# A trunk of two layers on one core: the recurrence's keys normed together behind its query projections, and the second layer's maps folded behind a feed-forward round

## The chip, the cores and the metric

The kernel runs on one core of one Trainium2 chip. The metric is the device time of one execution in microseconds. Names used here: PE is TensorE, DVE is VectorE, ACT is ScalarE, POOL is GpSimd, and SP is SyncE, whose queue issues nearly all transfers. L425 is line 425 of the kernel before.

## The reference, cut to what matters

Input is one sequence of 512 tokens of width 1024. Layer 0 norms it and projects it once; the columns go to a sparse attention (an indexer scores all keys and keeps the best 128 per query) and to a recurrence (RWKV-7). The part that is moved here belongs to the recurrence:

```
u = token_shift(u, mu)
r, k, v, xw, xa, xg = _split_cols(u, B_COLS)
a = jax.nn.sigmoid(a0 + xa @ a2)
kk = heads(k * k_k)
kk = kk / jnp.maximum(jnp.linalg.norm(kk, axis=-1, keepdims=True), 1e-12)
k = k * (1.0 + (a - 1.0) * k_a)
```

Here r are the recurrence's queries, k its keys and v its values, 512 columns each, in 8 heads of 64. A delta rule over the tokens follows. The two mixers' results are concatenated and projected, and a SwiGLU feed-forward and a per-layer embedding follow. Layer 1 has another mixer (mLSTM): an up-projection, a convolution over four tokens, small block-diagonal maps to queries, keys and values, and gates that are linear in those. The maps and the gates' weights multiply into combined maps that depend on weights alone. Layer 1 has a feed-forward and an embedding of its own.

## The kernel before, in words

Activations are kept turned, as 128 features by 512 tokens, one tile per 128 features, in an arena of 69 equal buffers that are handed out first in, first out (take, takes, give). A projection (project, L206 on) makes one tile of 128 outputs: eight input tiles times three matmuls, 24 in all, because weights and activations are each split into a high and a low part and three of the four products are summed. For each four input tiles, weights (L176) loads 256 KB on SP into one of four buffers, ACT casts the high part (L182) and POOL or DVE subtracts it to get the low part (L183) in one of three buffers; it is POOL in the first layer's mixer and DVE in the feed-forward. DVE takes the result from PSUM (L425), and shifted (L428) adds the previous token with one ACT and one DVE operation (L432, L433).

in_proj (L437) runs the recurrence's preparation. Before the change it went through the four key tiles one by one, with the next tile's projection started ahead: key(j, ks), L480 to L501, squares the tile on ACT (L483), sums the squares of each head on PE, turns the sums (one copy, L277, and one transpose), takes the reciprocal root with two ACT functions and one refinement step on DVE (rsqrt_act, L252 to L257, on 128x8 values), spreads it over the head's 64 rows by an ACT copy and four PE transposes (spread, L281 on; the copy is L286), and multiplies on DVE (L494 to L497) while POOL makes other products (L493, L499, L500). When all four are done, pairs_ab (L749) multiplies keys and rates, sends the result through memory (16 writes on SP, L760, one read, L762), and solve (L764) inverts blocks with 30 dependent DVE operations. The four query tiles (r) were projected after the solve in the text, each used and given back at once (L524 to L528, with DVE's bonus product L527).

The selection of the best keys (choose, L594) is 16 rounds of two DVE operations (L600, L601) and a last comparison (L603) for each of three query tiles, with a much later priority: fillers. The first 24 rounds are free to run once the scores are there, the others stand behind the solve's last operation.

From there rwkv (L854) writes the order of PE's groups out by hand, with group and issue_after. Everywhere else the order on each engine is made by the framework's scheduler: it simulates the program with its own durations and takes, for each engine, the ready instruction with the earliest place in the text. The engines then run that order strictly. issue_after(ins) orders what a block issues on the engine of ins behind ins, and nothing on other engines.

fold_maps (L1139 to L1187) makes layer 1's combined maps: two loads on SP (L1145, L1147), two dozen DVE operations (L1154 to L1172), a write to memory and a read back (L1174, L1178), a split and two POOL masks. It is called from layer 0's feed-forward (ffn, L1417) ahead of its third round (j = 2), a round being a gate and an up projection, DVE's evacuations (L1426, L1428), their product (L1429) and its split (L187, L188).

The last group norm of the recurrence (r_norm, L1075 on) is among PE's hand-ordered groups; the first half of the output projection (mixes, with ya) runs around it, and the second half (out_proj, with yb) needs its result.

Of the kernel before, what the change touches and what calls it, by code (L numbers as in the profile page):

```python
# [9 lines left out]
F32 = mybir.dt.float32  # L10
F32R = mybir.dt.float32r
I32 = mybir.dt.int32
AF = mybir.ActivationFunctionType
OP = mybir.AluOpType
# [4 lines left out]
P = 128  # L19
# [7 lines left out]
NT = S // P  # L27
# [18 lines left out]
def tl(c, n=P):  # L46
    return slice(c * n, (c + 1) * n)


class Trunk:  # L50
# [386 lines left out]
    def in_proj(self, ikw, *iq):  # L437
        nc, a = self.nc, self.a
        lora = self.takes(2)
        nc.sync.dma_start(lora[0], a["lora_w"])  # L440
        nc.sync.dma_start(lora[1], a["lora_a"])
        g2 = self.take()
        nc.sync.dma_start(g2, a["g2"])

        self.ikw, self.iq = ikw, iq

        wa = self.shifted(12)
        nc.scalar.activation(wa[0:64], wa[0:64], AF.Tanh)
        self.scores()
        xg = self.shifted(13)  # L450
        sg, av = self.takes(4), self.takes(4)
        sigmoids = []
        for j in range(4):
            ps = self.aux("decay")
            nc.tensor.matmul(ps, lora[0][:, tl(j)], wa, start=True, stop=True)
            sigmoids.append(nc.scalar.activation(sg[j], ps, AF.Sigmoid, bias=self.vec("w0", j)))
            ps = self.aux("a")
            nc.tensor.matmul(ps, lora[1][:, tl(j)], wa, start=True, stop=True)
            sigmoids.append(nc.scalar.activation(av[j], ps, AF.Sigmoid, bias=self.vec("a0", j)))
        sigmoids.append(nc.scalar.activation(xg, xg, AF.Sigmoid))  # L460

        with ExitStack() as ctx:
            for i in sigmoids:
                ctx.enter_context(self.tc.issue_after(i.ins))
            last = nc.scalar.preload_act_table_set("natural_log_exp_and_others")
        self.give(*lora, wa)
        inv = self.takes(4)
        dec = sg
        for j in range(4):
            nc.vector.tensor_tensor_scan(sg[j], self.reset, sg[j], 0.0, OP.mult, OP.add)  # L470
        with self.tc.issue_after(last.ins):
            for j in range(4):
                nc.scalar.activation(inv[j], sg[j], AF.Exp, scale=EXP_HALF)
                nc.scalar.activation(dec[j], sg[j], AF.Exp, scale=-EXP_HALF)
                nc.scalar.copy(self.PL[:, :, j], dec[j].rearrange("p (n t) -> p n t", t=64)[:, :, 63])
        self.give(self.reset)

        self.KK, self.Bt, self.Kt = [], [], []

        def key(j, ks):  # L480
            d3 = dec[j].rearrange("p (n t) -> p n t", t=64)
            sq = self.take()
            nc.scalar.activation(sq, ks, AF.Square, scale=self.vec("kk", j))  # L483
            ps = self.sums([[sq[:, tl(c)]] for c in range(NT)], self.heads)
            self.give(sq)
            v = self.sm.tile([P, 8], F32, name="kkv", tag="kkv")
            nc.vector.tensor_scalar(v.rearrange("p (c n) -> p c n", n=2), ps[:, :, :2], 1e-24, None, op0=OP.max)
            pb = self.spread(self.rsqrt_act(v, 8, "rk").rearrange("p (c n) -> p c n", c=NT), nc.scalar.copy)
            kk, bt, kt = self.takes(3)
            self.KK.append(kk)  # L490
            self.Bt.append(bt)
            self.Kt.append(kt)
            nc.gpsimd.tensor_tensor(bt, av[j], inv[j], op=OP.mult)  # L493
            nc.vector.scalar_tensor_tensor(kk, pb, self.vec("kk", j), ks, op0=OP.mult, op1=OP.mult)  # L494
            nc.vector.tensor_tensor(bt, kk, bt, op=OP.mult)
            k3 = kk.rearrange("p (n t) -> p n t", t=64)
            nc.vector.tensor_tensor(k3[:, :, 1:], k3[:, :, 1:], d3[:, :, :-1], op=OP.mult)  # L497
            nc.vector.tensor_scalar(av[j], av[j], self.vec("ka", j), self.ka1[:, j:j + 1], op0=OP.mult, op1=OP.add)
            nc.gpsimd.tensor_tensor(av[j], av[j], ks, op=OP.mult)  # L499
            nc.gpsimd.tensor_tensor(kt, av[j], inv[j], op=OP.mult)  # L500
            self.give(ks)  # L501

        ks = self.shifted(4)
        for j in range(4):
            k, ks = ks, self.shifted(5 + j) if j < 3 else None
            key(j, k)
        self.give(*inv)
        self.pairs_ab()

        self.kept = kept = []  # L510
        last = self.solve()
        with self.later(LATER):
            for c in range(1, NT):
                for i in range(17):
                    if (c, i) < (2, 8):
                        self.choose(c, i)
                    else:
                        with self.tc.issue_after(last.ins):
                            self.choose(c, i)
        self.kept = None  # L520
        keys = self.keys_in()
        next(keys)

        for j in range(4):  # L524
            rs = self.shifted(j)
            nc.gpsimd.tensor_tensor(self.Rt[:, j], rs, dec[j], op=OP.mult)
            nc.vector.scalar_tensor_tensor(self.bonus[:, j], rs, self.vec("rk", j), av[j], op0=OP.mult, op1=OP.mult)  # L527
            self.give(rs)  # L528
            if j == 1:
                next(keys, None)  # L530
        self.give(*dec, *av)
        vs = [self.shifted(8 + j) for j in range(4)]

        for j in range(4):
            gp = self.aux("gate")
            nc.tensor.matmul(gp, g2[:, tl(j)], xg, start=True, stop=True)
            bp = self.aux("bonus")
            bo, gate = self.bonus[:, j], self.gate[:, j]
            nc.tensor.matmul(bp, self.hblk, bo, start=True, stop=True)
            nc.vector.tensor_tensor(bo, bp, vs[j], op=OP.mult)  # L540
            nc.scalar.copy(gate, gp)
            nc.vector.scalar_tensor_tensor(bo, bo, self.vec("gnb", j), gate, op0=OP.add, op1=OP.mult)
            nc.scalar.mul(gate, gate, self.vec("gng", j))
        self.give(xg, g2)

        self.V = []
        for c in range(NT):
            ps = self.aux("vtok")
            for j in range(4):
                nc.tensor.matmul(ps[:, tl(j)], vs[j][:, tl(c)], self.center, start=True, stop=True)  # L550
            self.V.append(self.take())
            nc.scalar.copy(self.V[c], ps)
        self.give(*vs)
        self.give(*kept)
        self.q = [self.taken(17 + i) for i in range(4)]
# [861 lines left out]
    def ffn(self, i, after):  # L1417
        nc, a = self.nc, self.a
        h = []
        for j in range(NH):  # L1420
            if (i, j) == (0, 2):
                self.fold_maps()
            pg = self.project(a["ffn_w_gate"][i, j], self.xhi, self.xlo)
            pu = self.project(a["ffn_w_up"][i, j], self.xhi, self.xlo)
            gt, ut = self.takes(2)
            nc.vector.tensor_tensor(gt, pg, self.rstd, op=OP.mult)  # L1426
            nc.scalar.activation(gt, gt, AF.Silu)
            nc.vector.tensor_tensor(ut, pu, self.rstd, op=OP.mult)  # L1428
            nc.vector.tensor_tensor(ut, ut, gt, op=OP.mult)  # L1429
            hi, lo = self.pair("h")  # L1430
            self.split(hi, lo, ut)
            self.give(gt, ut)
            h.append((hi, lo))
        self.norm_done()
        self.norm_begin()
        for m in range(KD):
            ps = self.project(a["ffn_w_down"][i, m], *zip(*h))
            nc.vector.tensor_tensor(self.x[m], self.x[m], ps, op=OP.add)
            self.norm_tile(m, after)
        self.norm_end()  # L1440
        for hl in h:
            self.give(*hl)
# [169 lines left out]
```

## Time and profile before

| what | us |
|---|---|
| median of 3 runs | 1614.05 |
| lowest and highest | 1612.14, 1614.37 |
| the profiled execution's own time | 1613.23 |
| its span, first to last instruction | 1611.1 |

How it is read: the page's first part gives each engine's busy share of the span. A table of stretches gives the same for parts of the span, with TensorE's mean granted clock (1.00 is 2.4 GHz, 0.50 is 1.2 GHz). The view of waits says which engine idled, at which line, and what released it. The timeline lists instructions in order of time, each with the idle time ahead of it in brackets and what ended it. In all views, out<-in are the names of the tiles written and read; "t" is any arena tile.

### The profile page before, as it was taken

To read this page: it belongs to the slowest core of one execution; us is meant where nothing else is said; L and a number is where in the kernel's file an instruction comes from. 1 tells how busy PE (TensorE), PEld (TensorE's weight loads), DVE (VectorE), ACT (ScalarE), POOL (GpSimd) and SP (SyncE) were. 2 spreads that over 40 slices of the span, in tenths; PEclk is the share of its full clock that TensorE was granted. 3 is DMA by queue.
4 is the path that set the end of the run, shared out by engine and by line. 5 is a ranking of instruction groups with operands and counts; after the bars stand their busy time and mean duration, and the time that the engine had idled before them with its cause. 6 is when DMAs were issued, how large, how long until landed. Compare 5 with 4: busy or idle time off the path is not lost.

```text
span 1611.1 us, 25318 instructions
## 1 busy us (share of the span) xinstructions
PE 1540.2 (96%) x9814; PEld 1245.3 (77%) x9814; DVE 940.0 (58%) x1733; ACT 679.7 (42%) x1242; POOL 309.0 (19%) x288
## 2 busy tenths in 40 slices
PE   8789989989999999999999999999899999999998
PEld 5566767868888888888777777777788888888887
DVE  6988946576444443336676666657655444443345
ACT  5643446534333333334454655354453333333233
POOL 5545220121000000002300325353420000000002
PEclk9999999999999999999999999999999999999999
DMA  4124120222333333343322113121233333333332
GB/s 160 53 53 143 49 68 16 75 81 94 99 98 97 96 96 108 105 119 127 107 90 81 52 54 104 53 70 50 65 105 94 97 98 98 99 92 98 98 99 98
DMA packets 90112, 142.46 MB, mean 88 GB/s; under 512 B 19588, under 2 KB 24708, under 8 KB 89992
## 3 DMA queue, kind: packets, MB, share of 16 engines
q1 hardware_dynamic: 89992, 140.84, 28.6%
q8 instruction: 77, 1.26, 0.3%
q14 instruction: 43, 0.35, 0.1%
HBM read 133.26 MB, written 7.54 MB: 87 GB/s over the span
## 4 chain that ended last, share of the span: by engine, by line
PE 79%; DVE 16%; ACT 2%; issue 2%; DMA 1%; POOL 1%; SPq 0%; DVEq 0%; ACTq 0%; POOLq 0%
PE mm L145 66%; DVE t L601 2%; DVE m L600 1%; DVE t L1399 1%; PE s L145 1%; PE spread L148 1%; PE S L1320 1%; PE num L1367 1%; PE S L1321 1%; PE S L1319 1%; PE num L1368 1%; PE num L1369 1%; PE v L1353 1%; POOL t L1482 1%; PE po L145 1%
## 5 line engine op out<-in xcount | busy, mean ns | idle before, releaser
L145 PE MATMUL mm<-x,whi 128*128 128x512 f32 (+1 forms) x2496 | 780.4, 393 | 3.3 <-ACT x L308 3.3
L145 PEld LDWEIGHTS mm<-x,whi 128*128 128x128 f32 x2496 | 467.9, 189 | 105.7 <-issue 4.7
L182 ACT CAST whi<-wraw 128x512 fp32r<-128x512 f32 (+1 forms) x470 | 284.0, 606 | 572.2 <-PE mm L145 517.2
L145 PE MATMUL mm<-x,wlo 128*128 128x512 f32 (+1 forms) x1248 | 489.7, 392 | 3.4 <-POOL wlo L183 3.4
L183 DVE TENSOR_TENSOR wlo<-wraw,whi 128x512 fp32r<-128x512 f32 x352 | 245.4, 697 | 248.1 <-ACT whi L182 247.6
L145 PEld LDWEIGHTS mm<-x,wlo 128*128 128x128 f32 x1248 | 236.4, 189 | 53.5 <-POOL wlo L183 4.9
L183 POOL TENSOR_TENSOR wlo<-wraw,whi 128x512 fp32r<-128x512 f32 (+1 forms) x118 | 154.6, 1315 | 342.9 <-ACT whi L182 334.6
L145 PE MATMUL mm<-h,whi 128*128 128x512 f32 x704 | 216.8, 389 | 0.0
L318 POOL TENSOR_TENSOR t<-t 128x512 f32<-128x512 f32 x42 | 56.9, 1356 | 759.6 <-ACT t L317 759.3
L145 PEld LDWEIGHTS mm<-h,whi 128*128 128x128 f32 x704 | 132.2, 188 | 27.5
L145 PE MATMUL mm<-h,wlo 128*128 128x512 f32 x352 | 136.9, 389 | 0.0
L145 PE MATMUL mm<-y,whi 128*128 128x512 f32 x256 | 82.8, 402 | 2.8 <-DVE t L1410 2.8
L145 PEld LDWEIGHTS mm<-h,wlo 128*128 128x128 f32 x352 | 66.1, 188 | 13.6
L1428 DVE TENSOR_TENSOR t<-mm,t 128x512 f32<-128x512 f32 x44 | 30.4, 692 | 67.1 <-PE mm L145 67.1
L1426 DVE TENSOR_TENSOR t<-mm,t 128x512 f32<-128x512 f32 x44 | 30.4, 692 | 66.2 <-PE mm L145 64.6
L145 PEld LDWEIGHTS mm<-y,whi 128*128 128x128 f32 x256 | 49.0, 193 | 13.3 <-ACT whi L182 3.2
L187 ACT CAST h<-t 128x512 fp32r<-128x512 f32 x44 | 27.3, 620 | 64.9 <-DVE t L1429 64.9
L145 PE MATMUL mm<-y,wlo 128*128 128x512 f32 x128 | 50.9, 398 | 0.0
L309 DVE SCALAR_TENSOR_TENSOR x<-t,vecs,x 128x512 fp32r<-128x512 f32 x48 | 39.0, 815 | 19.2 <-ACT x L308 19.2
L188 DVE TENSOR_TENSOR h<-t,h 128x512 fp32r<-128x512 f32 x44 | 30.5, 693 | 30.0 <-ACT h L187 29.9
L308 ACT ACTIVATE x<-t,vecs 128x512 fp32r<-128x512 f32 x48 | 34.8, 725 | 27.6 <-POOL t L1482 15.5
L1214 DVE SCALAR_TENSOR_TENSOR t<-t,vecs 128x511 f32<-128x511 f32 (+2 forms) x48 | 35.7, 749 | 6.1 <-ACT t L1212 5.2
(363 smaller groups left out, 1853.2 us busy)
## 6 DMA issues: line engine op xcount, KB each, us to landing
wraw<-in_ffn_w_gate_dram SPq DMA_DIRECT2D x88, 256.0 KB, 2.6
wraw<-in_ffn_w_up_dram SPq DMA_DIRECT2D x88, 256.0 KB, 2.6
wraw<-in_ffn_w_down_dram SPq DMA_DIRECT2D x80, 256.0 KB, 2.6
wraw<-in_c_w_up_dram SPq DMA_DIRECT2D x64, 256.0 KB, 2.6
wraw<-in_w_in_dram SPq DMA_DIRECT2D x38, 256.0 KB, 2.6
wraw<-in_ple_w_gate_dram SPq DMA_DIRECT2D x32, 256.0 KB, 2.6
wraw<-in_c_w_down_dram SPq DMA_DIRECT2D x32, 256.0 KB, 2.7
t<-in_x_dram SPq DMA_DIRECT2D x16, 256.0 KB, 4.5
```

The source lines that it names most:

```text
L145: self.last = self.nc.tensor.matmul(*args, **kw)
L182: nc.scalar.copy(hi, raw)
L183: self.wlo_engine.tensor_tensor(lo, raw, hi.bitcast(F32), op=OP.subtract)
L187: self.nc.scalar.copy(hi, src)
L188: self.nc.vector.tensor_tensor(lo, src, hi.bitcast(F32), op=OP.subtract)
L308: nc.scalar.activation(hi, self.x[m], AF.Identity, scale=g)
L309: nc.vector.scalar_tensor_tensor(lo, self.x[m], g, hi.bitcast(F32), op0=OP.mult, op1=OP.subtract)
L318: nc.gpsimd.tensor_tensor(self.acc, self.acc, sq, op=OP.add)
L601: nc.vector.match_replace(acc, m8, acc, TAKEN)
L1214: nc.vector.scalar_tensor_tensor(xc[:, k:], xm[:, :-k], self.vec("cw", 16 * (3 - k) + i), xc[:, k:], op0=OP.mult, op1=OP.add)
L1426: nc.vector.tensor_tensor(gt, pg, self.rstd, op=OP.mult)
L1428: nc.vector.tensor_tensor(ut, pu, self.rstd, op=OP.mult)
```

## The change

The keys' four tiles are projected one after the other. Their squares are taken together, summed into one PSUM tile, and turned once, after the first query's projection. One reciprocal root of 128x32 values follows, and then two more query projections. Only then come the four spreads, with the products of each key as before. The fourth query's projection stands after them, ahead of the pairs. The four query tiles are held until all are used. Second, the block that calls fold_maps is put behind the last product of the feed-forward's second round (j = 1), so that its DVE operations may not be scheduled before it; its transfers and its ACT and POOL operations are not bound by that.

```
--- before.py
+++ after.py
@@ -477,34 +477,36 @@
 
         self.KK, self.Bt, self.Kt = [], [], []
 
-        def key(j, ks):
+
+        ks = [self.shifted(4 + j) for j in range(4)]
+        sqs = self.takes(4)
+        for j in range(4):
+            nc.scalar.activation(sqs[j], ks[j], AF.Square, scale=self.vec("kk", j))
+        sums = self.sums([[sq[:, tl(c)] for sq in sqs] for c in range(NT)], self.heads, turned=False)
+        self.give(*sqs)
+        rs = [self.shifted(0)]
+        sums = self.turned(sums)
+        v = self.sm.tile([P, 32], F32, name="kkv", tag="kkv")
+        nc.vector.tensor_scalar(v.rearrange("p (c n) -> p c n", n=8), sums[:, :, :8], 1e-24, None, op0=OP.max)
+        v = self.rsqrt_act(v, 32, "rk").rearrange("p (c n) -> p c n", c=NT)
+        rs += [self.shifted(1), self.shifted(2)]
+        for j in range(4):
             d3 = dec[j].rearrange("p (n t) -> p n t", t=64)
-            sq = self.take()
-            nc.scalar.activation(sq, ks, AF.Square, scale=self.vec("kk", j))
-            ps = self.sums([[sq[:, tl(c)]] for c in range(NT)], self.heads)
-            self.give(sq)
-            v = self.sm.tile([P, 8], F32, name="kkv", tag="kkv")
-            nc.vector.tensor_scalar(v.rearrange("p (c n) -> p c n", n=2), ps[:, :, :2], 1e-24, None, op0=OP.max)
-            pb = self.spread(self.rsqrt_act(v, 8, "rk").rearrange("p (c n) -> p c n", c=NT), nc.scalar.copy)
+            pb = self.spread(v[:, :, 2 * j:2 * j + 2], nc.scalar.copy)
             kk, bt, kt = self.takes(3)
             self.KK.append(kk)
             self.Bt.append(bt)
             self.Kt.append(kt)
             nc.gpsimd.tensor_tensor(bt, av[j], inv[j], op=OP.mult)
-            nc.vector.scalar_tensor_tensor(kk, pb, self.vec("kk", j), ks, op0=OP.mult, op1=OP.mult)
+            nc.vector.scalar_tensor_tensor(kk, pb, self.vec("kk", j), ks[j], op0=OP.mult, op1=OP.mult)
             nc.vector.tensor_tensor(bt, kk, bt, op=OP.mult)
             k3 = kk.rearrange("p (n t) -> p n t", t=64)
             nc.vector.tensor_tensor(k3[:, :, 1:], k3[:, :, 1:], d3[:, :, :-1], op=OP.mult)
             nc.vector.tensor_scalar(av[j], av[j], self.vec("ka", j), self.ka1[:, j:j + 1], op0=OP.mult, op1=OP.add)
-            nc.gpsimd.tensor_tensor(av[j], av[j], ks, op=OP.mult)
+            nc.gpsimd.tensor_tensor(av[j], av[j], ks[j], op=OP.mult)
             nc.gpsimd.tensor_tensor(kt, av[j], inv[j], op=OP.mult)
-            self.give(ks)
-
-        ks = self.shifted(4)
-        for j in range(4):
-            k, ks = ks, self.shifted(5 + j) if j < 3 else None
-            key(j, k)
-        self.give(*inv)
+        self.give(*ks, *inv)
+        rs.append(self.shifted(3))
         self.pairs_ab()
 
         self.kept = kept = []
@@ -522,13 +524,11 @@
         next(keys)
 
         for j in range(4):
-            rs = self.shifted(j)
-            nc.gpsimd.tensor_tensor(self.Rt[:, j], rs, dec[j], op=OP.mult)
-            nc.vector.scalar_tensor_tensor(self.bonus[:, j], rs, self.vec("rk", j), av[j], op0=OP.mult, op1=OP.mult)
-            self.give(rs)
+            nc.gpsimd.tensor_tensor(self.Rt[:, j], rs[j], dec[j], op=OP.mult)
+            nc.vector.scalar_tensor_tensor(self.bonus[:, j], rs[j], self.vec("rk", j), av[j], op0=OP.mult, op1=OP.mult)
             if j == 1:
                 next(keys, None)
-        self.give(*dec, *av)
+        self.give(*dec, *av, *rs)
         vs = [self.shifted(8 + j) for j in range(4)]
 
         for j in range(4):
@@ -1419,14 +1419,16 @@
         h = []
         for j in range(NH):
             if (i, j) == (0, 2):
-                self.fold_maps()
+
+                with self.tc.issue_after(mark.ins):
+                    self.fold_maps()
             pg = self.project(a["ffn_w_gate"][i, j], self.xhi, self.xlo)
             pu = self.project(a["ffn_w_up"][i, j], self.xhi, self.xlo)
             gt, ut = self.takes(2)
             nc.vector.tensor_tensor(gt, pg, self.rstd, op=OP.mult)
             nc.scalar.activation(gt, gt, AF.Silu)
             nc.vector.tensor_tensor(ut, pu, self.rstd, op=OP.mult)
-            nc.vector.tensor_tensor(ut, ut, gt, op=OP.mult)
+            mark = nc.vector.tensor_tensor(ut, ut, gt, op=OP.mult)
             hi, lo = self.pair("h")
             self.split(hi, lo, ut)
             self.give(gt, ut)
```

## Rows read from the trace of the kernel before

**Rows 1.** Page, part 1: busy us, share of the span and instructions of each engine
```profile
PE 1540.2 (96%) x9814; PEld 1245.3 (77%) x9814; DVE 940.0 (58%) x1733; ACT 679.7 (42%) x1242; POOL 309.0 (19%) x288
```

**Rows 2.** Stretches: from:to, length, busy of PE, PEld, DVE, ACT, POOL, clock, DMA
```profile
53.80:109.90 56.10, 43.37 (x243) 31.37 (x241) 53.05 (x116) 26.46 (x55) 31.59 (x27) 0.91 0.17 52
109.90:130.40 20.50, 19.89 (x169) 16.00 (x169) 13.05 (x17) 9.73 (x25) 12.58 (x10) 1.00 0.46 117
130.40:151.20 20.80, 19.74 (x87) 15.59 (x86) 20.08 (x40) 5.81 (x10) 9.97 (x7) 1.00 0.33 101
151.20:194.90 43.70, 39.59 (x167) 28.92 (x165) 42.41 (x90) 18.94 (x35) 15.60 (x16) 0.96 0.26 73
...
339.70:350.30 10.60, 5.40 (x19) 4.35 (x18) 9.22 (x30) 2.44 (x8) 0.60 (x1) 0.68 0.16 49
...
397.30:408.20 10.90, 10.90 (x50) 9.03 (x49) 5.19 (x9) 3.73 (x6) 0.00 (x0) 1.00 0.30 98
```

**Rows 3.** Waits of PE, 50 to 200 us: total us, times, longest
```profile
PE spread L148 <- ACT t L286: 9.2, 4, 4.6
...
PE sums L145 <- ACT t L483: 1.4, 1, 1.4
```

**Rows 4.** Timeline of DVE and PE at the end of the mixer
```profile
342.33 0.16 DVE L1084 TENSOR_SCALAR var<-sums 128x8 f32<-128x8 f32 x1
...
344.28 1.09 PE L148 MATMUL spread<-ident,t 128*128 128x128 f32 x4 [4.55 <-DVE t L286]
...
350.29 0.71 PE L145 MATMUL mm<-yb,whi 128*128 128x512 f32 x2 [0.65 <-DVE t L1103]
```

**Rows 5.** DVE by line, 46 to 110 us: count, busy us, mean ns, idle before
```profile
L601 DVE MATCH_REPLACE8 t<-m,t 128x256 f32<-128x256 f32 (+1 forms) x24 | 10.8, 451 | 0.0
L497 DVE TENSOR_TENSOR t<-t 128x504 f32<-128x504 f32 x4 | 5.3, 1318 | 0.0
...
L433 DVE SCALAR_TENSOR_TENSOR t<-t,vecs 128x511 f32<-128x511 f32 x5 | 4.1, 822 | 0.0
L257 DVE SCALAR_TENSOR_TENSOR rt_y<-rt_t,rt_y 128x8 f32<-128x8 f32 x4 | 4.0, 1002 | 0.0
L256 DVE TENSOR_TENSOR rt_t<-rt_t,rt_h 128x8 f32<-128x8 f32 x4 | 3.5, 876 | 0.0
```

**Rows 6.** Timeline of DVE and POOL: a key's root, and one alone
```profile
74.55 1.26 POOL L499 TENSOR_TENSOR t<-t 128x512 f32<-128x512 f32 x1
74.66 1.17 DVE L256 TENSOR_TENSOR rt_t<-rt_t,rt_h 128x8 f32<-128x8 f32 x1
...
343.28 0.17 DVE L256 TENSOR_TENSOR rt_t<-rt_t,rt_h 128x8 f32<-128x8 f32 x1
```

**Rows 7.** Timeline of DVE and SP up to the solve; the read's landing
```profile
109.19 0.68 DVE L497 TENSOR_TENSOR t<-t 128x504 f32<-128x504 f32 x1
...
122.39 0.33 SPq L762 DMA_DIRECT2D big<-ab  x1
...
DMA to landing us min/median/max: 4.6/4.6/4.6
...
128.55 1.89 DVE L527 SCALAR_TENSOR_TENSOR bonus<-t,vecs 128x512 f32<-128x512 f32 x1
130.36 1.24 DVE L775 TENSOR_TENSOR big<-big,big 128x2 f32<-128x2 f32 x1
```

**Rows 8.** DVE by line, 330.5 to 351 us: count, busy us, mean ns, idle before
```profile
L1159 DVE TENSOR_TENSOR t<-t 128x128 f32<-128x128 f32 x12 | 4.6, 441 | 3.2 <-DMA t<-in_c_qkv_dram 3.1
...
L1154 DVE TENSOR_REDUCE t<-t 128x128 f32<-128x512 f32 (+1 forms) x4 | 2.5, 617 | 0.1
```

**Rows 9.** Feed-forward timeline, DVE and PE; SP's waits, 320 to 380 us
```profile
428.66 0.69 DVE L183 TENSOR_TENSOR wlo<-wraw,whi 128x512 fp32r<-128x512 f32 x1
...
433.30 0.61 PE L145 MATMUL mm<-x,whi 128*128 128x512 f32 x2
...
SPq L179 <- DVE t L1171: 5.1, 1, 5.1
```

## What the change was predicted to do, before it ran

> **What bounds the kernel now.** I read the page's busy shares first, then the stretches of the first layer, then the waits and the queues inside the two stretches that the change touches. TensorE (PE) is busy 96% of the span [rows 1]: time can be won only where PE idles or runs at the lower of its two clock levels, and lost by making it do so elsewhere. Six stretches carry the argument [rows 2]. I cut them at the first matmul of the keys' first projection (53.8), the last key product on VectorE (DVE; 109.9), the solve's first and last operation (130.4, 151.2) and the recurrence's own products (194.9); a fifth holds the end of the mixer, a sixth one feed-forward round. In the first, PE is busy 43.4 of 56.1 us at a mean granted clock of 0.91, so about a fifth of it ran at 1.2 GHz, while DVE is busy 53.1 of 56.1: two near-bounds at once. From 151.2 to 194.9 DVE is the fuller one (42.4 of 43.7). PE's waits are mainly for the keys' normalisation: 9.2 us in four waits for the copy that feeds a key's spread, 1.4 us for a key's squares [rows 3]. The second place is the end of the mixer: there the fold's work stands on DVE's in-order queue, and PE idles 4.55 us before a spread [rows 4]. At 2.4 GHz the feed-forward round of 48 matmuls takes 10.9 us [rows 2], so a matmul steps by 0.227 us and a projection of 24 takes 5.45.
>
> **Part one, the keys.** Gone: three of four chains of row copy, transpose, maximum, Ln, Exp and four small root operations. On PE, ACT and POOL these are tenths of a microsecond in engines with room in that stretch [rows 2], priced at nothing; uncovered they would be about 1 us. On DVE they are not small: L256 and L257 took 3.5 and 4.0 us for four keys [rows 5], where the same 128x8 operation took 0.17 at 343.28 [rows 6]. At 74.66 one took 1.17 and ended with a POOL product that had begun just before it [rows 6]. Removing three of four saves between 1.0 us (six at 0.17) and 5.6 us (three quarters of 7.5); I take 3, about the middle, because POOL's products stay and will meet something else. The Trainium skill, SBUF — State Buffer, section "SBUF: two separate sides", says that a VectorE operation with two SBUF inputs and a GpSimd operation take a shared port pair as an exclusive lock, the other being fully blocked; by that the waits would only move to other DVE products, the saving would be the 1.0, and the total 2 us more.
>
> Moved ahead: the query projections, which stood behind the pairs of keys. Three of them come before the spreads; each brings a DVE evacuation (0.68, as a product of that size [rows 7]) and a shift (0.82 [rows 5]), 4.5 us together; the attention keys' projection, which PE had pulled forward, falls back (-0.7). DVE's need up to the last key is 53.1 - 3 + 4.5 - 0.7 = 53.9 us: as good as no change. But 24 rounds of selection lie in that stretch as fillers, their replacing halves alone 10.8 us [rows 5], and two or three can slide behind the last key into the 7.5 us that DVE idles from 109.9 to 130.4 [rows 2]. On PE, seven projections are 38.2 us, with about 2.4 for a late low part and the sums, so the spreads begin at 94.4 if they stand where they are written; four keys then take three DVE products each (0.68 twice [rows 7] and 1.32 [rows 5], 2.7 us) behind a first spread of 0.7, which ends at 106. Between this and 109.9 I take 107.9: **2.0 us gained**. Ends: 7 gained (every wait filled) and 12 lost (a rival below).
>
> POOL's products of rate and key no longer wait for a root and come earlier; POOL is busy 31.6 of 56.1 [rows 2] and low parts pass between them: nothing, or 1.3 us for one caught behind. SP issues the same weight loads in another order through the same four buffers: nothing, or one landing of some 3 us if a load came late. The arena gives out as many buffers as before.
>
> Behind the last key the pairs go through memory: the read is issued at 122.39 and lands 4.6 later, at 127.0, yet the solve starts at 130.36, behind a bonus product of 1.89 and what preceded it [rows 7]. With the queries done these are gone: **2.6 us gained** (0, if the values' shifts take the place, to 3.3). Another bonus product stands inside the solve: **1.8** (0 to 2). From there to 194.9 I take **1.5**, one evacuation with its shift done earlier (0 to 4). Part one: 7.9 us, bounds -12 and +14.
>
> **Part two, the fold.** On DVE the last group norm's root starts at 342.33 without a wait of its own [rows 4]: it stood in the queue, among the fold's operations. Without them the 4.55 us of PE's idle goes. So does the lower clock behind it (granted 0.68 in that stretch [rows 2]): from 344.28 to the next wait, at 349.64, PE needs 5.4 us [rows 4] for four transposes, eleven matmuls and two small ones, which at 2.4 GHz are about 3.1; 2.3 gained. Late next is the split of that norm's result, so of the 0.65 us wait [rows 4] I count half. **7.2 us gained** (4 to 7.5).
>
> The fold's price in the feed-forward: its DVE operations are 4.6 + 2.5 us [rows 8] and about 1.8 of smaller ones, 8.9. A round there leaves DVE 10.9 - 5.2 = 5.7 us [rows 2], so two rounds hold it, but it may go only behind the product of the second round and is written ahead of the third round's work. A low part ends at 429.35, and the matmuls that need it start at 433.30: 4.0 us of cover [rows 9]. If one low part waits for the whole block, PE stalls 4.9 us, and, as after the 4.55, runs at 1.2 GHz for another 2.3: 7.2 at worst. If low parts slip between its dependent steps, nothing. I take **1.5 lost**, nearer to nothing, since other work got between its steps at the end of the mixer, the root of 342.33 itself. SP is passed too: the fold's write waits for DVE's last copy, and a weight load stood 5.1 us behind it [rows 9]; loads are issued well ahead of their use, so nothing, or up to 3 us on top of the worst stall. ACT's one copy and POOL's two masks there lie in idle time.
>
> **The sum.** The profiled execution took 1613.23 (span 1611.1), 0.8 below the median of the three runs. 1613.2 - 7.9 - 7.2 + 1.5 = 1599.6; with the 0.8 back, **1600**. About 0.2%, 3.2 us, is what a measurement of this kernel can tell from no change.
>
> **Rivals**, each reckoned on the profiled execution.
> *The keys hide nothing (1607).* The queues' order is the scheduler's, not the text's: the fold ran in the mixer though written in the feed-forward. It puts the queries where they fill nothing, DVE stays the bound and only bare operations are saved: 1613.2 - 1.0 - 5.7. For it: DVE at 95% and 97% in two stretches [rows 2]. Against it: DVE's idle between 109.9 and 130.4. The lock rule of the Trainium skill's SBUF — State Buffer leads here.
> *PE recovers everything (1591).* All 10.6 us of waits for copies and squares [rows 3] and some 4 us of matmuls at 1.2 GHz pass through to the recurrence: 1613.2 - 14.6 - 7.2. For it: nearly every later stretch is PE-bound. Against it: DVE must keep pace.
> *The fold starves PE (1605).* The block delays a low part by its full length and part two nets nothing: 1613.2 - 7.9. For it: the fold is written ahead of the third round's low parts. Against it: the gaps between its dependent steps.
> *Slower: the spreads stand too late on PE (1621).* PE is in order. Each projection put ahead of the spreads costs 5.45 us at the last key product: with seven 106, with nine 117, with eleven 128. It decides from ten, where that product comes after 120: then the loss of 10 equals the 4.4 gained around the solve and the fold's 5.7. With eleven, 1613.2 + 17.9 - 4.4 - 5.7 = 1621. For it: a later projection had been pulled ahead before. Against it: the spreads are written behind three queries, and all four become ready at once.
>
> **The numbers.** Both parts pay 0.47 (own range 1594 to 1605), keys hide nothing 0.20, fold starves PE 0.13, PE recovers everything 0.10, slower 0.10. Faster by over 0.2% (under 1610.8): the first and the fourth whole and three quarters of the second and third, 0.81 rounded. Within 0.2%: the rest of those two and a little of the slower case, 0.10. Slower: 0.09. The range leaves out the slower case and the better half of the best one: 1591 to 1611.
>
> **What would show it.** Right: one root chain of 128x32 instead of four of 128x8; no wait of PE above 2 us for a spread's copy; the last key product by 109 and the solve's start by 127; the recurrence's first products by 188; at the end of the mixer no idle before the last spread and a granted clock of 1.00; the fold behind the feed-forward's second round, with PE's waits there under 2 us. Wrong: pairs of keys after 115, selection rounds pushed into the recurrence with PE waiting on them, a stall with clock 0.5 in the feed-forward, or fold operations still in the mixer.

## The result, and the profile after

The changed kernel takes 1629.54 us (median of 4 runs, 1627.07 to 1631.07), the kernel before, on the same chip, 1613.42 (4 runs, 1612.14 to 1614.37): a ratio of 1.0099 [1.0081, 1.0116]. It is slower by 16 us; 1600 had been forecast, in a range that ended at 1611. The profiled execution took 1628.64 (span 1626.8).

The page's first part of the changed kernel, the answer to [rows 1]:

```profile
PE 1565.3 (96%) x9811; PEld 1242.9 (76%) x9811; DVE 932.0 (57%) x1721; ACT 679.5 (42%) x1233; POOL 308.6 (19%) x285
```

PE has three matmuls fewer and is busy 25.1 us longer. Is it one place, or the whole span? The table of stretches, changed kernel (from:to, length, busy of PE, PEld, DVE, ACT, POOL, clock, DMA share, GB/s):

```profile
53.00:96.00 43.00, 37.42 (x180) 27.79 (x179) 40.52 (x95) 21.98 (x42) 32.52 (x25) 1.00 0.21 62
96.00:130.00 34.00, 31.51 (x240) 24.24 (x240) 20.95 (x26) 13.69 (x28) 14.80 (x11) 0.85 0.34 82
...
300.00:345.00 45.00, 44.33 (x665) 35.76 (x665) 25.20 (x57) 17.75 (x44) 8.70 (x8) 1.00 0.18 56
610.00:1540.00 930.00, 908.87 (x4360) 724.47 (x4360) 500.96 (x834) 379.93 (x636) 164.53 (x125) 0.99 0.29 88
```

and the same table for the kernel before:

```profile
53.00:96.00 43.00, 33.52 (x149) 24.15 (x148) 40.34 (x90) 21.50 (x45) 24.94 (x22) 0.88 0.16 49
96.00:130.00 34.00, 30.15 (x264) 23.25 (x263) 26.16 (x44) 15.49 (x37) 18.82 (x16) 1.00 0.36 93
130.00:192.00 62.00, 56.83 (x241) 42.70 (x240) 60.12 (x123) 23.76 (x41) 23.55 (x18) 0.97 0.29 84
192.00:237.00 45.00, 36.79 (x1021) 29.93 (x1022) 23.97 (x73) 23.94 (x65) 12.31 (x24) 0.96 0.23 76
...
610.00:1540.00 930.00, 908.75 (x4433) 740.45 (x4432) 507.42 (x843) 383.87 (x645) 165.76 (x126) 0.99 0.30 89
```

Read the last rows first. The 930 us from 610 to 1540 hold layer 1 and the end of layer 0, which the change does not touch. PE is busy as long in both (908.9 and 908.8 us), at the same clock of 0.99, yet gets through 73 matmuls fewer. The single matmul has become slower. The costliest groups on the page of the kernel before (count, busy us, mean ns of one):

```profile
L145 PE MATMUL mm<-x,whi 128*128 128x512 f32 (+1 forms) x2496 | 780.4, 393 | 3.3 <-ACT x L308 3.3
...
L145 PE MATMUL mm<-h,whi 128*128 128x512 f32 x704 | 216.8, 389 | 0.0
```

and of the changed one:

```profile
L145 PE MATMUL mm<-x,whi 128*128 128x512 f32 (+1 forms) x2496 | 791.8, 397 | 2.4 <-ACT x L308 2.1
...
L145 PE MATMUL mm<-h,whi 128*128 128x512 f32 x704 | 221.4, 396 | 0.0
```

Matmuls overlap, so what counts is the step from one start to the next. In PE's timeline a unit of three (two with the high weights, one with the low) repeats. Kernel before, in layer 1's feed-forward:

```profile
1300.05 0.62 PE L145 MATMUL mm<-x,whi 128*128 128x512 f32 x2
1300.51 0.39 PE L145 MATMUL mm<-x,wlo 128*128 128x512 f32 x1
1300.73 0.62 PE L145 MATMUL mm<-x,whi 128*128 128x512 f32 x2
```

Changed kernel:

```profile
1299.72 0.63 PE L145 MATMUL mm<-x,whi 128*128 128x512 f32 x2
1300.19 0.40 PE L145 MATMUL mm<-x,wlo 128*128 128x512 f32 x1
1300.42 0.63 PE L145 MATMUL mm<-x,whi 128*128 128x512 f32 x2
```

Three steps take 0.68 us before and 0.70 after. Over all 1054 adjacent pairs of matmuls on h tiles (the feed-forward's products) the mean step is 226.7 ns before and 233.3 after, where it alternates between 230 or 231 and 235 or 236. From the last yb matmul to the first on h (layer 0's feed-forward and embedding) the changed kernel needs 247.8 us and the first experiment's, which repairs this, 240.9; from there to the last on h, 965.5 and 947.8. That is 24.6 us in stretches where the two run the same instructions in the same order; the mixer, by contrast, ended 3.7 us sooner in the changed kernel's execution.

What the change was meant to do it did in part. PE's waits from 50 to 200 us, the answer to [rows 3]:

```profile
PE mm L145 <- POOL wlo L183: 3.1, 3, 1.4
PE bonus L539 <- DVE bonus L540: 3.1, 1, 3.1
PE sums L145 <- ACT t L484: 2.4, 1, 2.4
...
PE pair L145 <- DVE t L504: 1.8, 3, 0.9
...
PE spread L148 <- DVE t L286: 1.0, 1, 1.0
```

The 9.2 us for the spreads' copies are 1.0. The end of the mixer in the timeline, the answer to [rows 4]:

```profile
334.07 0.16 DVE L1084 TENSOR_SCALAR var<-sums 128x8 f32<-128x8 f32 x1
...
336.17 0.60 PE L148 MATMUL spread<-ident,t 128*128 128x128 f32 x4
...
340.47 0.70 PE L145 MATMUL mm<-yb,whi 128*128 128x512 f32 x2 [0.67 <-DVE t L1103]
```

The 4.55 us ahead of the last spread are gone, and the clock from 300 to 345 is 1.00. The fold runs behind the feed-forward's second round, in DVE's lines from 380 to 402 us (as [rows 8]):

```profile
L1159 DVE TENSOR_TENSOR t<-t 128x128 f32<-128x128 f32 x12 | 4.0, 398 | 0.0
...
L1154 DVE TENSOR_REDUCE t<-t 128x128 f32<-128x512 f32 (+1 forms) x4 | 2.4, 608 | 0.0
```

PE has no wait at all from 360 to 600 us. Only ahead of the solve did things come later, and not sooner (timeline, as [rows 7]):

```profile
132.23 0.33 SPq L762 DMA_DIRECT2D big<-ab  x1
...
141.11 1.22 DVE L775 TENSOR_TENSOR big<-big,big 128x2 f32<-128x2 f32 x1
```

### The profile page after: what moved, and what is told of

It reads as the page before. It is cut to its first block, busy times and chain, and to the rows that moved or that the text cites. A ratio compares the mean times of both kernels' runs of the same rounds, so it can differ in the third digit from the quotient of the medians.

```text
span 1626.8 us, 25291 instructions
## 1 busy us (share of the span) xinstructions
PE 1565.3 (96%) x9811; PEld 1242.9 (76%) x9811; DVE 932.0 (57%) x1721; ACT 679.5 (42%) x1233; POOL 308.6 (19%) x285
## 4 chain that ended last, share of the span: by engine, by line
PE 82%; DVE 14%; ACT 1%; issue 1%; DMA 0%; POOL 0%; SPq 0%; DVEq 0%; ACTq 0%; POOLq 0%
PE mm L145 69%; DVE t L601 1%; DVE m L600 1%; DVE t L1399 1%; PE s L145 1%; PE num L1367 1%; PE S L1320 1%; PE S L1321 1%; PE S L1319 1%; PE num L1368 1%; PE num L1369 1%; PE po L145 1%; PE v L1353 1%; PE pt L148 1%; PE pair L145 1%
## 5 line engine op out<-in xcount | busy, mean ns | idle before, releaser
L145 PE MATMUL mm<-x,whi 128*128 128x512 f32 (+1 forms) x2496 | 791.8, 397 | 2.4 <-ACT x L308 2.1
L145 PE MATMUL mm<-x,wlo 128*128 128x512 f32 (+1 forms) x1248 | 495.0, 397 | 3.1 <-POOL wlo L183 3.1
L145 PE MATMUL mm<-h,whi 128*128 128x512 f32 x704 | 221.4, 396 | 0.0
L145 PEld LDWEIGHTS mm<-h,whi 128*128 128x128 f32 x704 | 132.4, 188 | 31.9
```

The costliest lines, as they stand in the source:

```text
L145: self.last = self.nc.tensor.matmul(*args, **kw)
```

## The experiments

**Where the 22 us are.** The change widens one small tile: kkv has 32 floats per partition in place of 8, in two buffers, so 192 bytes more. The arena lies behind that pool, and its 69 buffers are multiples of 256 bytes. By the program's layout the arena starts at byte 46112 before and 46304 after, 32 and 224 modulo 256; the split weights' buffers stay at 31008, 32 modulo 256. The tile that a matmul streams in thus lay at a distance of 0 from its weights, modulo 256, and lies at 192. First run: the changed kernel with another small tile 32 bytes longer in two buffers, so that the distance is 0 again and the order of instructions is the same.

```
-        rows = self.sm.tile([P, P], F32, name="rows", tag="rows")
+        rows = self.sm.tile([P, P + 8], F32, name="rows", tag="rows")[:, :P]
```

> The changed kernel with the tile named rows 32 bytes wider in each of its two buffers, so that every arena tile lies 64 bytes further on: 256 bytes from its place before the change instead of 192. The order of instructions is that of the changed kernel. Theory (placement): the change widened a small tile, moved the arena by 192 bytes, and every matmul of 512 columns that streams an arena tile steps by 233.3 ns instead of 226.7; with the place restored up to a multiple of 256 the step is 226.7 again and the some 5000 matmuls give back 30 to 37 us, so about 1595, faster than before the change. Rival (the order itself): the slower step comes from the new order of instructions or from another stream on the chip; then the step stays 233.3 and the time 1629.

Measured: 1607.01 us (5 runs, 1605.79 to 1608.87), ratio to the kernel before 0.9963 [0.9949, 0.9977]. 64 unused bytes bring back 22.5 us. The step is 226.7 ns again, as expected; the time is not, since 30 to 37 us had been expected from it. The stretch of 930 us holds as many matmuls as before the change:

```profile
610.00:1540.00 930.00, 907.86 (x4434) 740.07 (x4434) 505.45 (x841) 383.41 (x645) 165.97 (x126) 0.99 0.29 89
```

The converse: the kernel before, moved by 192 bytes with the same tile (`P + 24`), nothing else.

> The kernel before the change with the tile named rows 96 bytes wider in each of its two buffers, so that the arena lies 192 bytes further on, as in the changed kernel, and nothing else differs. Placement theory: the step of the long matmuls goes from 226.7 to 233.3 ns everywhere and the time from 1613 to about 1642 (some 5000 matmuls by 6.6 ns, less a little in the stretches that PE does not bound). Rival (the order itself): step and time as before, 1613.

Measured: 1637.24 us (1635.81 to 1638.94), ratio 1.0149 [1.0134, 1.0164]; the step is 233.3 ns. It is 24.5 us, where about 29 had been expected. The slowdown is made by the place alone, without any of the change:

```profile
610.00:1540.00 930.00, 909.21 (x4370) 722.54 (x4370) 504.17 (x839) 380.75 (x639) 162.85 (x124) 1.00 0.29 88
```

**Own place or distance?** In the next kernel the first 40 arena buffers are 32 bytes longer, so that tiles start at all eight multiples of 32 modulo 256 while the weights stay.

```
-        t = slot[0].tile([P, S], dt, name=name, tag=slot[1], bufs=1)
+        k = 8 if slot[1] in STAGGER else 0
+        t = slot[0].tile([P, S + k], dt, name=name, tag=slot[1], bufs=1)[:, :S]
```

> The kernel before the change with the first 40 of the arena's 69 buffers made 32 bytes longer each, so that the buffers lie at all eight multiples of 32 modulo 256. Placement theory: the step of a matmul depends on where the tile that it streams begins; sorted by that start modulo 256 the steps fall into two or more levels, 226.7 at 32 and 233.3 at 224 among them. If a start at a multiple of 64 or 128 is quicker than both, a level near 216 shows there. Rival: the steps do not depend on the start, all 226.7.

Measured: 1628.32 us (one run), steps mostly from 224 to 240 ns, their means between 230 and 233 at every start, 230.1 even between two tiles that both start like the weights (1591 pairs). Neither the expectation nor its rival came true: a tile's own start does not sort the steps. Where the six matmuls ahead of such a pair start like the weights too, the mean is 227.8 (332 pairs). So what was streamed shortly before may count as well; neighbouring matmuls have different distances here, and no run isolates this.

So the weights were moved and the arena left. In the kernel before, the weights' tiles are 576 wide, and a round of the feed-forward uses them from an offset of its own: 32 bytes more each round in layer 0 (from 0 again after eight rounds), 16 in layer 1 (after sixteen), none elsewhere. Whole rounds have one distance.

```
+        k = self.woff
-        hi = self.wsp.tile([P, n], F32R, name="whi", tag="whi")
+        hi = self.wsp.tile([P, 576], F32R, name="whi", tag="whi")[:, k:k + n]
...
+            self.woff = 4 * (j % 16) if i else 8 * (j % 8)
```

> The kernel before the change; the streamed tiles start where they did (32 modulo 256), but the split weights' buffers are 2304 bytes long and the weights' place in them changes from round to round of the feed-forward: in layer 0 by 32 bytes a round over 0 to 224, in layer 1 by 16 bytes a round over 0 to 240. All else is as before (one small tile shares another's buffer). Theory A (the streamed tile's own place): the step is 226.7 ns in all rounds. Theory B (the distance between the streamed tile and the weights that are loaded beside it): the step changes from round to round, is 226.7 in rounds with the weights at 0, and 233.3 with the weights 64 bytes further on, where the distance is what it is in the changed kernel (192 modulo 256). If some distance gives less than 226.7, it is a way to a faster kernel.

Measured: 1622.66 us (one run). Mean step by distance (start of the streamed tile less that of the weights, modulo 256) in the gate and up projections, 47 to 235 pairs each:

| distance, bytes | mean step, ns |
|---|---|
| 240, 0, 16 | 226.7, 226.7, 227.1 |
| 32, 48, 64, 80 | 233.4, 233.3, 229.0, 229.9 |
| 96, 112, 128, 144 | 233.4, 233.4, 232.7, 233.3 |
| 160, 176 | 234.2, 231.8 |
| 192, 208, 224 | 233.3, 233.3, 233.3 |

Stretches of 50 us with PE busy throughout show it in the matmuls' counts: 650 to 700 and 1450 to 1500 are down-projections at distance 0, the others gate and up projections at changing distances:

```profile
450.00:500.00 50.00, 50.00 (x218) 40.48 (x217) 23.96 (x38) 16.70 (x28) 0.00 (x0) 1.00 0.28 95
650.00:700.00 50.00, 50.00 (x223) 41.39 (x222) 17.34 (x26) 15.31 (x27) 4.16 (x4) 1.00 0.35 101
1250.00:1300.00 50.00, 50.00 (x216) 40.28 (x215) 24.27 (x37) 16.86 (x27) 0.00 (x0) 1.00 0.29 96
1450.00:1500.00 50.00, 50.00 (x222) 41.37 (x222) 19.01 (x29) 16.19 (x27) 2.63 (x2) 1.00 0.33 95
```

The distance sorts the steps, in layer 0 and layer 1 alike: only within 16 bytes of 0 are they near 226.7. Neither place alone decides. Here the weights moved and the tiles stayed, in the run moved by 192 bytes it was the other way round, and at a distance of 192 both give 233.3. No run moved both by the same amount, which would test the distance by itself.

**The two parts by themselves.** The kernel before with the fold moved, whose layout is unchanged:

```
-                self.fold_maps()
+                with self.tc.issue_after(mark.ins):
+                    self.fold_maps()
```

> The kernel before the change with the fold alone put behind the feed-forward's second round; the arena stays where it was. Theory (both parts pay, the placement takes it back): the idle of 4.55 us before the last spread and the low clock behind it go, PE loses 0 to 3 us in the feed-forward, the step stays 226.7, and the time is 1606 to 1610. Rival (the fold starves PE in the feed-forward): 1613 or more.

Measured: 1605.64 us (1604.25 to 1607.01) against 1612.74, ratio 0.9953 [0.9938, 0.9967]: 7.1 us gained. By the trace the first yb matmul comes 6.6 us sooner, the first matmul on h 6.5: the feed-forward takes nothing back.

The keys' part alone, with the pad of the first experiment:

> The changed kernel without the fold's part (the fold is called as before the change), with the arena 256 bytes from its old place, so that the step should be 226.7 ns. Theory (the keys hide nothing): 1612 to 1616, no gain, since both parts at that place took 1607.0 and the fold alone 1605.6. Rival (the keys pay and the two parts get in each other's way): 1605 to 1609.

Measured: 1612.73 us (10 runs, 1611.08 to 1617.04) against 1612.34 (13 runs), ratio 1.0006 [0.9996, 1.0016]: worth nothing. The table of stretches of this kernel says where its gain went:

```profile
53.00:96.00 43.00, 37.04 (x177) 27.98 (x176) 38.99 (x93) 20.78 (x40) 32.38 (x25) 0.96 0.18 62
96.00:130.00 34.00, 30.18 (x236) 23.57 (x235) 21.96 (x25) 12.84 (x26) 14.56 (x11) 0.85 0.29 78
130.00:192.00 62.00, 57.82 (x247) 43.92 (x246) 53.81 (x108) 25.44 (x49) 21.19 (x21) 0.94 0.28 85
192.00:237.00 45.00, 37.66 (x1047) 30.44 (x1045) 30.60 (x94) 24.43 (x65) 10.77 (x20) 0.89 0.22 73
```

Take from each row PE's idle time (length less busy) and the time it lost to the lower clock (busy times 1 less the clock). Before, the four rows give 9.5 + 3.8 + 5.2 + 8.2 = 26.7 us idle and 4.0 + 0 + 1.7 + 1.5 = 7.2 lost; here 6.0 + 3.8 + 4.2 + 7.3 = 21.3 idle and 1.5 + 4.5 + 3.5 + 4.1 = 13.6 lost. 5.4 us of waiting are gone, and 6.4 us more are lost to the clock. These are single executions, but the other traces with a step of 226.7 agree. In the seven with the keys moved (those below included) the four rows give 21.2 to 23.4 us idle and 11.6 to 13.6 lost; in the three with the keys as before, 26.7 to 27.8 and 6.7 to 7.3. The changed kernel's own execution lost 6.1. The largest new loss follows the keys' products. PE's timeline there:

```profile
110.29 0.34 PE L145 MATMUL pair<-t 64*64 64x64 f32 x8 [1.04 <-DVE t L504]
111.86 0.34 PE L145 MATMUL pair<-t 64*64 64x64 f32 x8 [1.23 <-DVE t L504]
...
114.97 1.51 PE L145 MATMUL pair<-t 64*64 64x64 f32 x32 [0.90 <-DVE t L504]
...
122.26 1.05 PE L145 MATMUL mm<-x,whi 128*128 128x512 f32 x2
```

Two matmuls that span 0.62 us at 2.4 GHz span 1.05 at 122.26: from about 115 to 125 PE runs at 1.2 GHz, behind waits for single products of DVE. Before, the idle time from 96 to 130 us is as long (3.8 us), but lies apart, from 97 to 120, and the clock there is 1.00; here it stands within 6 us, while DVE goes through all four keys' products one behind the other, from 103.7 to 115.5.

**Trying to save the keys.** Two suspects stood in that trace beside the clock. DVE's 24 free selection rounds end at 88.8, it has 21.8 us of idle time from there to the end of the solve at 160.4, and the last of the other rounds comes at 214.6 instead of 197.0; and SP's read of the pairs is held from 125.7 to 133.5 behind weight loads. Both edits on the first experiment's kernel, alone and together, and the first of them on the kernel with only the fold moved:

```
-                    if (c, i) < (2, 8):
+                    if (c, i) < (3, 0):
...
-        nc.sync.dma_start(self.big[1][:, :1024], ab)
+        nc.scalar.dma_start(self.big[1][:, :1024], ab)
```

> The changed kernel with the arena put back by 64 bytes more, as in the first experiment, and with all rounds of the second query tile's selection free to run before the solve (32 of 48 instead of 24, with one more of the last comparisons). Theory (the keys' part gained nothing because VectorE ran out of free rounds at 88.8 us, idled some 15 us up to the solve's end, and the rounds that slid behind the solve, up to 214.6 us, took back the 2.5 us by which the recurrence starts sooner): the last round now comes 7 to 9 us earlier, near 206, and the gain at the recurrence's start of 3 to 4 us stays to the end of the mixer: about 1603 to 1605, ratio to before 0.994. Rival one (PE's own work bounds the mixer from the recurrence on, the rounds lie beside it): the last round comes earlier and the time stays at 1607, ratio 0.9963. Rival two (the freed rounds take VectorE from the keys' products): the last key product comes after 114.8 and the time is 1608 to 1611.

Measured: 1603.09 us (6 runs, 1600.38 to 1607.14; the kernel before on that chip 1613.01), ratio 0.9938 [0.9921, 0.9954]. The profiled execution is the longest of the six, and in it the last round comes at 193.2 where it had come at 216.1, yet the last of the recurrence's second half<-d group, a mark within the recurrence, starts at 237.2 as before (237.5). The mechanism that was expected is not in the trace: an earlier selection did not bring that mark sooner. The interval overlaps with that of the first experiment.

> The changed kernel with the arena put back, and with the one read of the pairs issued from ScalarE's queue and not from SP's, where it stood behind weight loads that wait for GpSimd's low parts. PE's order is the same. Theory (SP's queue holds the read from 125.7, when the last write is done, to 133.5, and the solve with it): the read is issued by 128 and the solve starts by 135 and not at 142.2, the recurrence's first product at 188 to 189. Whether the end follows is the question of the other experiments: 1604 to 1607 if a sooner recurrence stays won, 1607 if it is given back by 237 us as before. Rival (a projection's evacuation stands ahead of the solve on VectorE and waits for PE, so the read is not what binds): the solve stays within 3 us of 142.2 and the time at 1607.

Measured: 1604.64 us (1603.51 to 1605.65), ratio 0.9942 [0.9930, 0.9955]. The expectation failed: the read was issued later than on SP, at 136.5 (132.4 in the first experiment), behind ACT's other work. In the first experiment the read had landed at 136.8, yet the solve started at 141.1, behind a projection's result that DVE waited for; here it started at 139.9 and waited for the read itself. DVE's timeline in the first experiment:

```profile
140.48 0.69 DVE L425 TENSOR_TENSOR t<-mm,t 128x512 f32<-128x512 f32 x1 [2.46 <-PE mm L145]
141.09 1.22 DVE L775 TENSOR_TENSOR big<-big,big 128x2 f32<-128x2 f32 x1
```

and in this run:

```profile
139.90 0.16 DVE L775 TENSOR_TENSOR big<-big,big 128x2 f32<-128x2 f32 x1 [1.44 <-DMA big<-ab]
```

So SP's queue was not what the solve waited for, as the rival had it, but the time is 2 us under the rival's. The mark in the recurrence comes at 234.7. PE lost less to the clock from 192 to 237: 36.6 us busy at a clock of 0.92 are 2.9 us, and 37.9 at 0.78 were 8.3.

> Both of the two edits before in one kernel. If the keys' part lost its gain to the rounds that slid and to the read behind weight loads, each alone shows part and both together the whole of the 7.9 us foreseen less what PE's late spreads cost (about 4): 1602 to 1604, ratio 0.993. If the mixer is bound by PE from the recurrence on, this is again 1606 to 1608.

Measured: 1603.67 us (1601.81 to 1604.47), ratio 0.9935 [0.9922, 0.9948]. The time is what was expected if both suspects had eaten the gain, but the traces of the two runs before show neither at work. Of the kernels in this part it is the only one whose interval lies below that of the first experiment (0.9949 to 0.9977), by a hair; with the fold alone it overlaps.

> The control: the kernel before with the fold moved (1605.6, ratio 0.9953) and the same eight more rounds free, without the change to the keys. There VectorE was busy 53.1 of 56.1 us up to the last key product, but idled 7.5 us from there to the solve. If free rounds are what the later stretch lacks whatever the keys do, this gains 2 to 4 us as well: 1602 to 1604. If they matter only behind the moved keys, or crowd VectorE ahead of the last key product, it stays at 1605.6 or loses 1 to 3 us.

Measured: 1605.42 us (1604.05 to 1608.77), ratio 0.9950 [0.9935, 0.9966], the same as without the edit (0.9953): the rounds are no lever where the keys stay as they were.

Last, GpSimd's twelve products of rates and keys out of the loop over the spreads and ahead of it, alone and with both other edits:

```
+        for j in range(4):
+            kk, bt, kt = self.takes(3)
...
+            nc.gpsimd.tensor_tensor(bt, av[j], inv[j], op=OP.mult)
         for j in range(4):
```

> The changed kernel with the arena put back, and with GpSimd's twelve products of rates and keys taken out of the loop over the spreads and issued ahead of it, so that none runs beside the keys' twelve products on VectorE. Theory (in the changed order those products are drawn out by GpSimd's, 3.42 us for two that take 1.26 alone, so PE waits 3.2 us for them at the pairs of keys and then runs at 1.2 GHz for some 10 us, which loses 4.7 us of matmul time between 96 and 130 us): the last key product comes 2 to 3 us earlier (112), PE's waits at the pairs are under 1.5 us, the time lost to the lower clock between 96 and 130 falls under 2 us, and the time to 1602 to 1605 (ratio 0.993 to 0.995). Rival one (PE idles there whatever GpSimd does, since twelve products behind one another take 11 us): the waits stay over 2.5 us and the clock falls as before: 1607. Rival two (what is won here is lost at the next lower clock, as the 2 to 4 us won at the recurrence's start were, with 9.2 us lost to the clock from 192 to 237): the waits fall and the time stays at 1606 to 1608.

Measured: 1604.94 us (8 runs, 1604.06 to 1609.63), ratio 0.9945 [0.9925, 0.9965]. PE's waits at the pairs stay (2.9 us for the same products, 3.2 with the keys alone), and so does the clock (4.6 us lost from 96 to 130): rival one, except that its time was 1607. The timeline of DVE and POOL in it shows why:

```profile
105.37 3.39 POOL L183 TENSOR_TENSOR wlo<-wraw,whi 128x512 fp32r<-128x512 f32 x2
...
105.88 3.42 DVE L506 TENSOR_TENSOR t<-t 128x504 f32<-128x504 f32 x2
...
111.75 1.27 DVE L506 TENSOR_TENSOR t<-t 128x504 f32<-128x504 f32 x2
```

What draws two products out from 1.27 to 3.42 us are low parts of weights on GpSimd, not the products that were moved. The Trainium skill, SBUF — State Buffer, section "SBUF: two separate sides", has a VectorE operation with two SBUF inputs and a GpSimd operation that reads SBUF exclude each other. These rows agree: the four operations take 3.93 us together, from 105.37 to 109.30, and one after the other they would take 3.92 (0.67 for each of DVE's, as at 112.34, and 1.29 for each low part, as at 101.82).

> The three edits in one kernel: GpSimd's products ahead, the second tile's selection rounds free, and the read of the pairs on ScalarE's queue. If PE's waits and the lower clock behind them are what ate the keys' gain, this is the fastest of all: 1599 to 1603, ratio 0.990 to 0.993. If each lower clock that is spared comes again a little later, it stays at 1603 to 1605 with the two edits alone.

Measured: 1602.25 us (6 runs, 1600.14 to 1609.24) against 1613.59, ratio 0.9928 [0.9902, 0.9953]. It is the best median and faster than the kernel before and the changed one, but its interval overlaps with that of the fold alone: whether the keys' part is worth 2 or 3 us with these edits stays open. What the expectation named as the reason did not happen either: PE still loses 12.5 us to the lower clock in the four stretches.

## Why the prediction was wrong

**The step that failed** is the one that costs memory: "The arena gives out as many buffers as before." It looked at the number of buffers, and not at where they start. The sum has no term for that, and none of the rivals does. Its size is +22.5 us (from the first experiment to the changed kernel) or +24.5 (the kernel before, moved). Without it the forecast of 1600 would have met 1607: inside its range, but with the keys' part wrong all the same.

**The keys, forecast at 7.9 us, measured 0.** The waits for the spreads went, as forecast. The terms behind them did not come: with the keys alone the last key product ended at 115.5 in place of the 107.9 forecast, and the solve started at 142.2 in place of 127. The spreads stood at 101.9 to 103.8 and not at 94.4: ahead of them PE waited 3.4 us for low parts and 2.5 for a key's squares, where 2.4 in all had been allowed for a low part and the sums. The twelve products then took 11.8 us. The recurrence's first products came at 192.4, 2.5 us sooner than in the execution before; but with the fold alone, where the keys are as before, they came at 192.4 too, so this difference cannot be put down to the keys. The later mark came at 236.0, against 237.2. The rival in which the keys hide nothing had the right sum, 1607, but not the cause: it held that queries would fill nothing, whereas PE's idle time did shrink, by 5.4 us, and by the traces the lower clock took it. The working gave the clock a term at the end of the mixer and none here. One of its sums is also off: the ends given with the four terms of the keys add up to 16.3 us at the better side, not 14.

**The fold, forecast at 7.2 less 1.5, measured 7.1** (5.3 to 10.0 by the interval). The 4.55 us of idle time and the clock behind it came back about as reckoned (the first yb matmul 6.6 us sooner); the 1.5 us for the feed-forward were not needed, since PE has no wait there at all. The two rivals in which the fold starves PE, or the spreads stand so late that the kernel gets slower, did not happen: the seven projections stood ahead of the spreads as written.

Shown by runs: the cost of the place, that neither the tiles' place nor the weights' decides it alone, and each part's worth. Read from the trace and not isolated by a run: that the lower clock behind the pairs and in the recurrence ate the keys' gain. Not tried: a kernel in which the waits at the pairs are gone.

## What to carry to other kernels

A change to the size of any tile moves what is allocated behind it. Compare the mean of the costliest matmul group in a stretch that the change does not touch before you explain anything else, and if it moved, put the layout back with a pad and measure again. And when a stall of PE is closed by reordering, count the idle time and the time at the lower clock together, over all stretches up to the next point where PE is full: here 5.4 us less of one came with 6.4 more of the other.

## What had not been expected of the hardware

The step of a matmul of 512 columns depends on where the streamed tile lies relative to the weights: 226.7 ns when their starts agree modulo 256 within 16 bytes, mostly 233 when not, 2.9% more, at a granted clock of 1.00 in both. What in the reading of the two collides is not shown; the run with staggered tiles suggests that neighbours with different distances mix their steps. The Trainium skill, SBUF — State Buffer, section "SBUF: two separate sides", says that PE never waits on anyone there; by these runs its step depends on the place all the same, and the measurement decides. The Trainium skill, TensorE: Matmul & The Clock Gate, section "Part 2: What happens when you issue a matmul", gives 215.7 ns for 512 columns back to back; no distance that was tried here had a mean step below 226.7.
